# Ten instead of eight seven-product quads in each sweep of the MLPs' second weights, with one weight sum made in DRAM

## The chip, the cores and the metric

The kernel runs on one core of a Trainium2 chip. A core has engines with instruction queues of their own: TensorE (PE, matmuls; PEld in the profile are its weight loads), VectorE (DVE), ScalarE (ACT), GpSimd (POOL) and SyncE (SP), which here only issues DMAs. They wait for one another through semaphores. The metric is the device time of one launch in microseconds (us), as the median of several runs.

## The reference

A trunk of two layers on 256 positions of width 2048, in float32. Layer 0 mixes along the sequence with a convolution module, layer 1 with latent attention, and each is followed by a squared-ReLU MLP with residual add:

```python
D_MODEL, SEQ, DEPTH, D_FF = 2048, 256, 2, 8192

def sq_relu_mlp(h, w1, w2):
    return jnp.square(jax.nn.relu(h @ w1)) @ w2

# per layer: x = x + mixer(rms_norm(x)); x = x + sq_relu_mlp(rms_norm(x), w1, w2)
# at the end: rms_norm(x)
```

w1 is 2048 x 8192 and w2 8192 x 2048, so the four products of the two MLPs are most of the work, and their 256 MB of float32 weights are streamed from DRAM once.

## The kernel before

**Products of float32.** TensorE multiplies in a rounded form of float32. Each operand is therefore split: hi is its rounding, formed by ScalarE (L169 and L431), and lo what is left over, formed by VectorE as a subtraction (L173 and L432). A product is three matmuls into one PSUM bank, hi x hi, lo x hi and hi x lo (`mm3`, L202 to L204): with a stationary sh, sl of the inputs and a moving hi, lo of the weights. The third one (L204) is the first that needs the weights' lo.

**The MLP.** Its 8192 inner columns are worked off in two halves (`hf`). A half has an up stage and two sweeps. The up stage has 8 groups of 512 inner columns; for each come four loads of 1 MB of w1 (four blocks of 128 rows x 512 columns), which makes 32 loads, or steps, a half. For each block there are four pairs of matmuls (L645 with hi, L646 with lo of the weights). After each group its four PSUM banks are squared and scaled and split to hi and lo: these become the inputs of the second product. They come in one of two shapes, for plain or for mixed quads.

**The sweeps.** A sweep (`n` = 0 or 2) multiplies the half's inputs, 256 positions x 4096, with 4096 x 1024 of w2. It has 16 quads: two blocks of rows of w2 by two blocks of 512 columns, a load of 1 MB. A *plain* quad is eight products (2 rows x 2 columns x 2 position blocks), 24 matmuls. A *mixed* quad computes the same with seven products, 21 matmuls (a scheme of Strassen's kind, in Winograd's form): sums of input blocks are formed once when the group is put away (`mixed_inputs`, L453 and L459 to L462), sums of weight blocks whenever a quad is loaded (`mixed_weights`: L439 makes two 512-column sums at once, L440 and L441 one each). All seven weight blocks are split to hi and lo. The products are added up over the quads of the sweep in eight PSUM banks, four for the plain results (e) and four for mixed sums (u). `join` takes the u banks apart at the end (L522 to L525) and `close` adds the e banks to the residual xs. In the first half xs is added to by accumulating DMAs that POOL issues (L512), in the second half by VectorE (L514, L535).

**What sets the order.** In the program, groups 0, 2, 4 and 6 of each half are mixed: eight mixed and eight plain quads a sweep. `HEAD` and `TAIL` say how many plain quads come ahead of the first and after the last mixed one. Each engine runs its own queue in order; that order is fixed when the program is built, by the tile framework's scheduler, from the program's order and its buffers. The buffers are rings: three raw tiles of 1 MB for loads, which SP issues as they come free (L159), and six hi and six lo tiles of half a load each (`WB`). The inputs of the up stage lie in the tiles xt.

## Time and profile before

| | |
|---|---|
| three runs | 1942.09, 1942.22, 1942.23 us; median 1942.22 |
| span of the profiled execution | 1940.9 us |
| busy: PE, DVE, ACT, POOL | 1920.0, 1604.5, 1095.4, 241.9 us |
| mean rate of the DMA engines | 193 GB/s |
| up stage, MLP 0, first half (its end) and second half | to 478 us, 641 to 818.6 us |
| two sweeps, MLP 0, first half | 478 to 559.5 and 559.5 to 641 us |
| two sweeps, MLP 0, second half | 818.6 to 899.7 and to 980.4 us |
| two sweeps, MLP 1, first half | 1424 to 1505.5 and to 1587 us |
| two sweeps, MLP 1, second half | 1764.7 to 1846 and to 1931.5 us |

The bounds of the stages are read from the first and last matmuls of their lines and then used as windows, so they are good to some tenths of a us. In rows of the timeline the first number is the start in us from the span's start and the second the length in us; one row can stand for several instructions (x2). A length counts from an instruction's start to the end of its last write, so two that follow each other overlap a little, and what an instruction costs in a row of others is the distance of the starts. An arrow `<-` stands between the tile written and those read, and in brackets stands the idle time before an instruction with what ended it.

### The profile page before, as it was taken

To read this page: it belongs to the slowest core of one execution; us is meant where nothing else is said; L and a number is where in the kernel's file an instruction comes from. 1 tells how busy PE (TensorE), PEld (TensorE's weight loads), DVE (VectorE), ACT (ScalarE), POOL (GpSimd) and SP (SyncE) were. 2 spreads that over 40 slices of the span, in tenths; PEclk is the share of its full clock that TensorE was granted. 3 is DMA by queue.
4 is the path that set the end of the run, shared out by engine and by line. 5 is a ranking of instruction groups with operands and counts; after the bars stand their busy time and mean duration, and the time that the engine had idled before them with its cause. 6 is when DMAs were issued, how large, how long until landed. Compare 5 with 4: busy or idle time off the path is not lost. (4 is left out here: it accounts for less than half of the span.)

```text
span 1940.9 us, 28606 instructions
## 1 busy us (share of the span) xinstructions
PE 1920.0 (99%) x10799; PEld 1683.0 (87%) x10799; DVE 1604.5 (83%) x2490; ACT 1095.4 (56%) x1636; POOL 241.9 (12%) x196
## 2 busy tenths in 40 slices
PE   8999999999999999999999999999999999999997
PEld 8999888888888888888889998888888888888876
DVE  7999988877999667799976766877789986778998
ACT  5667755555565455455666565555555555555655
POOL 6999200000010000000002310000000010000000
PEclk9999999999999999999999999999999999999999
DMA  7766456555576866555665445466546786555654
GB/s 230 212 188 182 156 192 209 186 192 174 190 233 222 249 191 195 174 183 201 204 197 149 141 135 192 155 214 194 185 163 224 221 268 198 185 187 186 224 184 142
DMA packets 214571, 373.93 MB, mean 193 GB/s; under 512 B 15896, under 2 KB 90912, under 8 KB 214176
## 3 DMA queue, kind: packets, MB, share of 16 engines
q1 hardware_dynamic: 209648, 363.28, 58.1%
q0 software_dynamic: 3456, 6.29, 1.8%
q10 hardware_dynamic: 1328, 2.52, 0.4%
q8 instruction: 84, 1.38, 0.3%
q14 instruction: 55, 0.45, 0.1%
HBM read 363.68 MB, written 2.10 MB: 188 GB/s over the span
## 5 line engine op out<-in xcount | busy, mean ns | idle before, releaser
L173 DVE TENSOR_TENSOR lo<-raw,hi 128x1024 fp32r<-128x1024 f32 (+2 forms) x503 | 598.5, 1204 | 249.1 <-ACT hi L169 245.6
L169 ACT ACTIVATE hi<-raw 128x1024 fp32r<-128x1024 f32 (+1 forms) x568 | 578.8, 1038 | 357.8 <-PE acc L645 212.6
L645 PE MATMUL acc<-xt,hi 128*128 128x512 f32 x2048 | 710.5, 390 | 0.0
L646 PE MATMUL acc<-xt,lo 128*128 128x256 f32 x2048 | 577.5, 282 | 0.0
L645 PEld LDWEIGHTS acc<-xt,hi 128*128 128x128 f32 x2048 | 384.4, 188 | 80.6
L646 PEld LDWEIGHTS acc<-xt,lo 128*128 128x128 f32 x2048 | 387.1, 189 | 0.2
L431 ACT ACTIVATE hi<-raw 128x1024 fp32r<-128x1024 f32 (+1 forms) x256 | 235.6, 947 | 233.5 <-DVE raw L439 151.5
L432 DVE TENSOR_TENSOR lo<-raw,hi 128x1024 fp32r<-128x1024 f32 (+1 forms) x256 | 271.9, 1086 | 22.4 <-ACT hi L431 18.1
L204 PE MATMUL acc<-lo,sh 128*128 128x512 f32 x512 | 199.6, 390 | 1.9 <-DVE lo L432 1.9
L204 PE MATMUL acc<-lo,gh 128*128 128x512 f32 (+1 forms) x516 | 199.9, 388 | 0.8 <-DVE lo L173 0.8
L202 PE MATMUL acc<-hi,gh 128*128 128x512 f32 (+1 forms) x516 | 200.0, 388 | 0.0
L203 PE MATMUL acc<-hi,gl 128*128 128x512 f32 (+1 forms) x516 | 199.9, 387 | 0.0
L202 PE MATMUL acc<-hi,sh 128*128 128x512 f32 x512 | 199.6, 390 | 0.2 <-ACT hi L431 0.2
L788 PE MATMUL acc<-xt,hi 128*128 128x256 f32 x1024 | 180.1, 281 | 0.3 <-ACT b L1070 0.2
L203 PE MATMUL acc<-hi,sl 128*128 128x512 f32 x448 | 174.3, 389 | 0.0
L875 DVE SCALAR_TENSOR_TENSOR sum<-ub,w_dw,sum 128x256 f32<-128x256 f32 x409 | 164.2, 480 | 3.5 <-ACT sum L845 3.0
L173 POOL TENSOR_TENSOR lo<-raw,hi 128x1024 fp32r<-128x1024 f32 x65 | 155.1, 2412 | 17.3 <-ACT hi L169 17.3
L788 PEld LDWEIGHTS acc<-xt,hi 128*128 128x128 f32 x1024 | 154.6, 188 | 1.1 <-ACT xt L1054 0.6
L788 PE MATMUL acc<-xt,lo 128*128 128x256 f32 x512 | 139.2, 279 | 0.0
L512 POOL DMA_DIRECT2D xs<-v x24 | 21.1, 961 | 882.7 <-DVE lo L173 701.5
L204 PEld LDWEIGHTS acc<-lo,sh 128*128 128x128 f32 x512 | 96.1, 188 | 23.2 <-DVE lo L432 3.2
L204 PEld LDWEIGHTS acc<-lo,gh 128*128 128x128 f32 x516 | 96.8, 188 | 21.1 <-DVE lo L173 1.3
(309 smaller groups left out, 2568.2 us busy)
## 6 DMA issues: line engine op xcount, KB each, us to landing
raw<-in_mlp_w SPq DMA_DIRECT2D x256, 1024.0 KB, 5.4
raw<-in_conv_w_pw SPq DMA_DIRECT2D x62, 512.0 KB, 5.1
raw<-in_conv_w_pw SPq DMA_DIRECT2D x16, 1024.0 KB, 5.0
raw<-in_mla_w_o SPq DMA_DIRECT2D x16, 1024.0 KB, 5.4
raw<-in_mla_w_kv_up SPq DMA_DIRECT2D x8, 1024.0 KB, 5.4
xs<-v POOLq DMA_DIRECT2D x24, 256.0 KB, 7.6
raw<-in_mla_w_in SPq DMA_DIRECT2D x8, 576.0 KB, 3.8
raw<-in_mla_w_in SPq DMA_DIRECT2D x4, 1024.0 KB
```

Source lines behind the costliest of these rows:

```text
L169: nc.scalar.activation(hi, raw[:, js, :], AF.Copy)
L173: eng.tensor_tensor(lo, raw, hi.bitcast(F32), op=ALU.subtract)
L202: nc.tensor.matmul(ps, sh, mh, start=start, stop=False)
L203: nc.tensor.matmul(ps, sl, mh, start=False, stop=False)
L204: nc.tensor.matmul(ps, sh, ml, start=False, stop=stop)
L431: nc.scalar.activation(hi, src, AF.Copy)
L432: nc.vector.tensor_tensor(lo, src, hi.bitcast(F32), op=ALU.subtract)
L512: nc.gpsimd.dma_start(x, o, accum_op=ALU.add)
L645: nc.tensor.matmul(ps[b], wh[:, bs], xhl(k), start=k == 0, stop=False)
L646: nc.tensor.matmul(ps[b][:, :S], wl[:, bs], xh(k), start=False, stop=k == KC - 1)
L788: nc.tensor.matmul(pss[c][b][:, :S], w[i][:, bs], (xh, xl)[j](k), start=k == i + j == 0, stop=end and k == k0 + nk - 1 and (i, j) == terms ...
L875: nc.vector.scalar_tensor_tensor(out=out, in0=ubs[c][:, w : w + S], scalar=tap(c, w), in1=base, op0=ALU.mult, op1=ALU.add)
```

## The change

In each half groups 0, 2, 4, 6 and 7 are mixed: ten mixed and six plain quads a sweep. What goes with it:

- **Names and signs.** The four weight sums are written so that the first, q1, is the sum of the top row's two column blocks. The others follow from it: q2 = q1 + lower right, q3 = q2 - upper left, q4 = q2 + lower left (L456 to L458 in the new file, 512 columns each). The signs of the input sums and of `join` change to match.
- **q1 in DRAM.** During the first 20 of a half's 32 up steps, SP copies the right block of a quad's top row (256 KB of w2) to a DRAM tile behind the step's weight load (`issue_after`), and one step later an accumulating DMA of POOL's adds the left block. That is done for both sweeps' ten mixed quads: 80 copies and 80 accumulating DMAs in all.
- **A mixed quad's load** is three DMAs into one raw tile, 1 MB together: q1 (256 KB), the lower row (512 KB), the upper left block (256 KB). The upper right block isn't loaded.
- **Three steps.** A first half (lower right block and q1) is split as soon as its two loads are there; then upper left and lower left, and the three sums; then q2 alone, and q3 with q4. The function `run` calls the next quad's first half between the sums and the last splits of the present one. The order of the seven products changes to fit. Plain quads are cut alike, their second half being the middle step.
- **Room.** Group 7's inputs lie in the third of the xt tiles, which is now 2 MB, as the up stage needs it no more then. In each MLP's first half the tile's contents are put aside in DRAM after group 1 and brought back in the second sweep. In that sweep group 7's quads come first.
- `HEAD` is (1, 1) in place of (2, 1).

```diff
-MIXED = {(0, 0): (0, 2, 4, 6), (0, 1): (0, 2, 4, 6), (1, 0): (0, 2, 4, 6), (1, 1): (0, 2, 4, 6)}
-N_MIXED = 4
-HEAD, TAIL, LAST_TAIL = (2, 1), 2, 3
+MIXED = (0, 2, 4, 6, 7)
+IN_XT = 7
+XT_PAD = 56
+HEAD, TAIL, LAST_TAIL = (1, 1), 2, 3
...
+    dram = ctx.enter_context(tc.tile_pool(name="dram", bufs=1, space=bass.MemoryType.DRAM))
...
+    def weight_load(dst, src):
+        last_load[0] = nc.sync.dma_start(dst, src)
...
-        xt[:] = [
-            pool.tile([P, KC // NNB, 2 * S], F32R, name=nm("xt")) for _ in range(NNB)
-        ]
-    xhl = lambda k: xt[k // 4][:, k % 4, :]
+        xt[:] = [pool.tile([P, n, 2 * S], F32R, name=nm("xt")) for n in (KC // 4, KC // 4, KC // 2)]
+    def xrows(k, n):
+        i = min(k // 4, 2)
+        return xt[i][:, k - 4 * i : k - 4 * i + n, :]
...
-    def mixed_weights(raw):
-        def halves(src):
+    class MixedWeights:
+        def __init__(self, w, k, n, q1):
+            top, low = (w[(k + i) * P : (k + i + 1) * P, n * NB : (n + 2) * NB] for i in range(2))
+            raw = self.raw = wpool.tile([P, 4, NB], F32, tag="raw", name=nm("raw"), bufs=3)
+            weight_load(raw[:, 3, :], q1)
+            weight_load(raw[:, 1:3, :], low.rearrange("p (c n) -> p c n", c=2))
+            weight_load(raw[:, 0, :], top[:, :NB])
+            self.b22, self.q1 = self.halves(2, 4)
+        def halves(self, a, b):
+            src = self.raw[:, a:b, :]
             hi = wpool.tile(list(src.shape), F32R, tag="hi", name=nm("hi"), bufs=WB)
             lo = wpool.tile(list(src.shape), F32R, tag="lo", name=nm("lo"), bufs=WB)
             nc.scalar.activation(hi, src, AF.Copy)
             nc.vector.tensor_tensor(lo, src, hi.bitcast(F32), op=ALU.subtract)
-            return [(hi[:, i, :], lo[:, i, :]) for i in range(src.shape[1])]
-        b11, b21 = halves(raw[:, :, :NB])
-        (b22,) = halves(raw[:, 1:2, NB:])
-        top = raw[:, 0, :].rearrange("p (c n) -> p c n", c=2)
-        low = raw[:, 1, :].rearrange("p (c n) -> p c n", c=2)
-        nc.vector.tensor_tensor(top, raw[:, :, NB:], top, op=ALU.subtract)
-        nc.vector.tensor_tensor(low[:, 1, :], low[:, 1, :], top[:, 0, :], op=ALU.subtract)
-        nc.vector.tensor_tensor(low[:, 0, :], low[:, 0, :], low[:, 1, :], op=ALU.subtract)
-        t1, t3 = halves(top)
-        t4, t2 = halves(low)
-        return b11, b21, b22, t1, t2, t3, t4
+            return [(hi[:, i, :], lo[:, i, :]) for i in range(b - a)]
+        def sums(self):
+            raw = self.raw
+            self.b11, self.b21 = self.halves(0, 2)
+            nc.vector.tensor_tensor(raw[:, 3, :], raw[:, 3, :], raw[:, 2, :], op=ALU.add)
+            nc.vector.tensor_tensor(raw[:, 0, :], raw[:, 3, :], raw[:, 0, :], op=ALU.subtract)
+            nc.vector.tensor_tensor(raw[:, 1, :], raw[:, 3, :], raw[:, 1, :], op=ALU.add)
+        def rest(self):
+            (self.q2,) = self.halves(3, 4)
+            self.q3, self.q4 = self.halves(0, 2)
+    class PlainWeights:
+        def __init__(self, w, k, n):
+            self.raw = load([rows(w, k, 2, n * NB, 2 * NB)], 2)
+            self.parts = [split_half(self.raw, 0, nc.vector)]
+        def sums(self):
+            self.parts.append(split_half(self.raw, 1, nc.vector))
+        def rest(self):
+            pass
+        def at(self, j):
+            return [a[:, 0, :] for a in self.parts[j]]
...
-        def mixed(self, w, k, fh, fl, end):
-            b11, b21, b22, t1, t2, t3, t4 = mixed_weights(load([rows(w, k, 2, self.n * NB, 2 * NB)], 2))
+        def mixed(self, b, fh, fl, end):
             u1, u6, u7, u5 = self.u
             work = [
-                (u1, 0, b11), (u5, 6, t1), (u7, 4, t3), (u6, 3, t2),
-                (self.e[0][0], 1, b21), (self.e[0][1], 5, b22), (self.e[1][0], 2, t4),
+                (self.e[0][1], 5, b.b22), (u5, 6, b.q1), (u1, 0, b.b11), (self.e[0][0], 1, b.b21),
+                (u6, 3, b.q2), (u7, 4, b.q3), (self.e[1][0], 2, b.q4),
             ]
-            if self.begun:
-                work = [work[i] for i in (0, 4, 5, 1, 2, 6, 3)]
             for ps, i, (wh, wl) in work:
                 mm3(ps, fh[:, i, :], fl[:, i, :], wh, wl, self.first(ps), end and any(ps is u for u in self.u))
...
+                ms = [(g, b) for g in mixed for b in range(2)]
+                sums_due = [(n, i) for n in range(0, NNB, 2) for i in range(len(ms))]
+                first_sums, half_done = {}, []
...
+                        while half_done:
+                            q1, src = half_done.pop(0)
+                            nc.gpsimd.dma_start(q1, src, accum_op=ALU.add)
+                        if sums_due:
+                            n, i = key = sums_due.pop(0)
+                            k = k_lo + 4 * ms[i][0] + 2 * ms[i][1]
+                            q1 = first_sums[key] = dram.tile([P, NB], F32, name=nm("q1"))
+                            row = w[k * P : (k + 1) * P, n * NB : (n + 2) * NB]
+                            with tc.issue_after(last_load[0].ins):
+                                nc.sync.dma_start(q1, row[:, NB:])
+                            half_done.append((q1, row[:, :NB]))
...
+                    if not last and g == 1:
+                        spare = dram.tile([P, KC // 2, 2 * S], F32, name=nm("spare"))
+                        nc.sync.dma_start(spare, xt[2].bitcast(F32))
...
+                    if g == IN_XT:
+                        room_x = xt[2].rearrange("p k n -> p (k n)")[:, XT_PAD : XT_PAD + 4 * 7 * P]
+                        gs[g] = [a.rearrange("p (b i n) -> p b i n", b=2, i=7) for a in (room_x[:, : 14 * P], room_x[:, 14 * P :])]
...
-                    g, b = ms[i]
-                    sums.mixed(w, k_lo + 4 * g + 2 * b, gs[g][0][:, b], gs[g][1][:, b], i == len(ms) - 1)
+                    n = sums.n
+                    at = i if n == 0 else (i - 2) % len(ms)
+                    g, b = ms[at]
+                    return (
+                        lambda: MixedWeights(w, k_lo + 4 * g + 2 * b, n, first_sums[n, at]),
+                        lambda q: sums.mixed(q, gs[g][0][:, b], gs[g][1][:, b], i == len(ms) - 1),
+                    )
+                def plain_quad(sums, k, at_end):
+                    def middle():
+                        while due:
+                            prepare(due.pop(0))
+                    return (
+                        lambda: PlainWeights(w, k_lo + k, sums.n),
+                        lambda q: sums.plain(q, hi, lo, k, at_end, middle if at_end else None),
+                    )
+                def run(units):
+                    quads = [u for u in units if isinstance(u, tuple)]
+                    begun = [quads[0][0]()]
+                    for u in units:
+                        if not isinstance(u, tuple):
+                            u()
+                            continue
+                        q = begun.pop()
+                        q.sums()
+                        quads.pop(0)
+                        if quads:
+                            begun.append(quads[0][0]())
+                        q.rest()
+                        u[1](q)
...
+                        if not last and n == NNB - 2 and i == len(ks) // 2:
+                            units.append(lambda: nc.sync.dma_start(xt[2].bitcast(F32), spare))
                         if i == len(ks) - tail + 1:
-                            sums.join(room)
-                        at_end = i == len(ks) - 1
-                        sums.plain(
-                            w, k_lo + k, hi, lo, k, at_end,
-                            (lambda: [prepare(due.pop(0)) for _ in range(len(due))]) if at_end else None,
-                        )
+                            units.append(lambda: sums.join(room))
+                        units.append(plain_quad(sums, k, i == len(ks) - 1))
                     if ends:
-                        while at < len(ms):
-                            mixed_quad(sums, at)
-                            at += 1
+                        units += [mixed_quad(sums, i) for i in range(at, len(ms))]
+                    run(units)
...
```

VectorE's order shows the weights of one mixed quad. Before, in the first half's first sweep of MLP 0 (raw_5649 is the quad's load; hi and lo are its split blocks):

```order
L432 TENSOR_TENSOR lo_5652<-raw_5649,hi_5651 128x1024
L432 TENSOR_TENSOR lo_5656<-raw_5649,hi_5655 128x512
L439 TENSOR_TENSOR raw_5649<-raw_5649 128x1024
L440 TENSOR_TENSOR raw_5649<-raw_5649 128x512
L441 TENSOR_TENSOR raw_5649<-raw_5649 128x512
L432 TENSOR_TENSOR lo_5663<-raw_5649,hi_5662 128x1024
L432 TENSOR_TENSOR lo_5667<-raw_5649,hi_5666 128x1024
```

Now, in the same sweep (raw_5716 is the quad, raw_5755 the next one, raw_5799 a plain one behind it):

```order
L450 TENSOR_TENSOR lo_5721<-raw_5716,hi_5720 128x1024
L450 TENSOR_TENSOR lo_5749<-raw_5716,hi_5748 128x1024
L456 TENSOR_TENSOR raw_5716<-raw_5716 128x512
L457 TENSOR_TENSOR raw_5716<-raw_5716 128x512
L458 TENSOR_TENSOR raw_5716<-raw_5716 128x512
L450 TENSOR_TENSOR lo_5760<-raw_5755,hi_5759 128x1024
L450 TENSOR_TENSOR lo_5764<-raw_5716,hi_5763 128x512
L450 TENSOR_TENSOR lo_5768<-raw_5716,hi_5767 128x1024
L450 TENSOR_TENSOR lo_5793<-raw_5755,hi_5792 128x1024
L456 TENSOR_TENSOR raw_5755<-raw_5755 128x512
L180 TENSOR_TENSOR lo_5802<-raw_5799,hi_5801 128x1024
```

Before, the quad's rows stand together. Now lo_5760, the next quad's first half, stands between its sums and its last two splits; three steps of 1024 columns are left (with L439 there were four) and four of 512 (there were three).

Behind the other kind of neighbour, a few quads on, the quad's own rows close up (raw_5755 of above, raw_5838 the next mixed one):

```order
L457 TENSOR_TENSOR raw_5755<-raw_5755 128x512
L458 TENSOR_TENSOR raw_5755<-raw_5755 128x512
L450 TENSOR_TENSOR lo_5806<-raw_5755,hi_5805 128x512
L450 TENSOR_TENSOR lo_5810<-raw_5755,hi_5809 128x1024
L180 TENSOR_TENSOR lo_5835<-raw_5799,hi_5834 128x1024
L450 TENSOR_TENSOR lo_5843<-raw_5838,hi_5842 128x1024
```

Here the 1024-column split, which reads what L457 and L458 write, follows L458 with only one 512-column row between.

SP's queue in the up stage of MLP 0's first half, before only the loads of L159, now (q_ are the DRAM sums, spare the tile put aside):

```order
L157 DMA raw_4047<-in_mlp_w 128x4x512
L691 DMA q_510_4090<-in_mlp_w 128x512
L157 DMA raw_4092<-in_mlp_w 128x4x512
L691 DMA q_516_4135<-in_mlp_w 128x512
L697 DMA spare_4227<-xt_100 128x4096
L157 DMA raw_4137<-in_mlp_w 128x4x512
L691 DMA q_522_4180<-in_mlp_w 128x512
```

A copy now stands behind each load, and once the 2 MB going out.

43 lines of the change are left out of this document (23 added, 20 removed).

## The prediction

> **What bounds the kernel now.** The kernel's profiled execution has a span of 1940.9 us, and the runs have a median of 1942.22 us, so 1.3 us lie around the span. I make the sum as a difference and add it to the median. The first view read is the page's table of busy times, and after it a table of stretches: the two sweeps of MLP 0's first half, the up stage and the two sweeps of its second half, and the kernel's last two sweeps. The columns are the length, then busy time of PE, PEld, DVE, ACT and POOL (with instructions), the granted clock, the DMA share and GB/s.
>
> ```profile
> PE 1920.0 (99%) x10799; PEld 1683.0 (87%) x10799; DVE 1604.5 (83%) x2490; ACT 1095.4 (56%) x1636; POOL 241.9 (12%) x196
> 478.00:559.50 81.50, 81.50 (x362) 67.52 (x361) 76.84 (x85) 45.93 (x53) 3.64 (x4) 1.00 0.60 194
> 559.50:641.00 81.50, 81.50 (x362) 67.49 (x361) 76.44 (x80) 46.97 (x52) 5.22 (x6) 1.00 0.74 236
> 641.00:818.60 177.60, 177.60 (x1026) 157.40 (x1025) 124.97 (x185) 90.02 (x127) 1.77 (x2) 1.00 0.64 200
> 818.60:899.70 81.10, 81.10 (x360) 67.17 (x359) 78.44 (x89) 45.71 (x53) 0.10 (x1) 1.00 0.56 189
> 899.70:980.40 80.70, 79.94 (x352) 65.53 (x351) 78.32 (x92) 46.08 (x57) 0.15 (x1) 1.00 0.60 198
> 1764.70:1846.00 81.30, 81.30 (x361) 67.35 (x360) 78.46 (x89) 45.18 (x52) 0.00 (x0) 1.00 0.60 201
> 1846.00:1931.50 85.50, 83.26 (x375) 68.09 (x373) 82.41 (x103) 47.50 (x62) 0.00 (x0) 1.00 0.47 159
> ```
>
> TensorE is the bound, at full clock. But the average of 83% for VectorE hides that in a sweep it works 76.4 to 78.5 us of 81.5: only 3 to 5 us are free. In the up stage it is free for 50 us of 177.6. So a cut of TensorE's sweeps is worth its full size only while VectorE keeps up. The timeline of TensorE shows where it already doesn't: single matmuls around the gaps in the second halves' second sweeps (start, length, and in brackets the idle time with its releaser).
>
> ```profile
> 912.09 0.39 PE L203 MATMUL acc<-hi,sl 128*128 128x512 f32 x1
> 912.32 0.39 PE L204 MATMUL acc<-lo,sh 128*128 128x512 f32 x1
> ...
> 914.20 0.50 PE L204 MATMUL acc<-lo,sh 128*128 128x512 f32 x1 [0.70 <-DVE lo L432]
> 914.54 0.40 PE L202 MATMUL acc<-hi,sh 128*128 128x512 f32 x1
> ...
> 1858.37 0.39 PE L204 MATMUL acc<-lo,sh 128*128 128x512 f32 x1
> ...
> 1860.69 0.40 PE L202 MATMUL acc<-hi,sh 128*128 128x512 f32 x1
> 1875.22 0.39 PE L203 MATMUL acc<-hi,sl 128*128 128x512 f32 x1
> 1876.14 0.50 PE L204 MATMUL acc<-lo,sh 128*128 128x512 f32 x1 [0.54 <-DVE lo L432]
> 1876.48 0.40 PE L202 MATMUL acc<-hi,sh 128*128 128x512 f32 x1
> 1922.11 0.39 PE L204 MATMUL acc<-lo,gh 128*128 128x512 f32 x1
> 1923.32 0.73 PE L204 MATMUL acc<-lo,gh 128*128 128x512 f32 x2 [0.83 <-DVE lo L173]
> 1923.89 0.40 PE L202 MATMUL acc<-hi,gh 128*128 128x512 f32 x1
> ```
>
> Matmuls of 512 columns start 0.226 us apart where nothing waits (81.5 us over 360 of them; 912.09 to 912.32). From 912.32 to 914.54 four steps took 2.22 us instead of 0.91: 1.3 lost. In the last sweep 1858.37 to 1860.69 lost 1.4, 1875.22 to 1876.48 lost 0.8, and 1922.11 to 1923.89 1.1. In all 4.6 us, each after a late lo of VectorE.
>
> **Term 1: matmuls.** Ten quads of 21 matmuls and six of 24 make 354 where eight and eight made 360: 6 fewer, 6 x 0.2264 = 1.36 us per sweep, and 8 sweeps give **-10.9 us**. A sweep falls to 80.1 us.
>
> **Term 2: VectorE's weights.** The timeline of VectorE over one mixed and one plain quad, in a sweep in which it hardly waits:
>
> ```profile
> 847.38 1.22 DVE L439 TENSOR_TENSOR raw<-raw 128x1024 f32<-128x1024 f32 x1
> 848.63 0.69 DVE L440 TENSOR_TENSOR raw<-raw 128x512 f32<-128x512 f32 x1
> 849.35 0.69 DVE L441 TENSOR_TENSOR raw<-raw 128x512 f32<-128x512 f32 x1
> 849.96 2.52 DVE L432 TENSOR_TENSOR lo<-raw,hi 128x1024 fp32r<-128x1024 f32 x2
> 852.40 2.35 DVE L173 TENSOR_TENSOR lo<-raw,hi 128x1024 fp32r<-128x1024 f32 x2
> 854.67 1.82 DVE L432 TENSOR_TENSOR lo<-raw,hi 128x1024 fp32r<-128x1024 f32 x2
> 856.40 1.22 DVE L439 TENSOR_TENSOR raw<-raw 128x1024 f32<-128x1024 f32 x1
> L431 ACT ACTIVATE hi<-raw 128x1024 fp32r<-128x1024 f32 x192 | 200.9, 1057 | 230.6 <-DVE raw L439 151.5 <-DVE raw L441 33.7 <-PE acc L203 24.2
> ```
>
> A plain quad takes 2.27 us (852.40 to 854.67, so 1.14 a subtraction of 1024), a mixed and a plain one 9.02 (847.38 to 856.40), so the mixed one 6.75; a 512-wide step takes 0.6 (1.73 - 1.14). A mixed quad of the change has three of 1024 and four of 512: 3 x 1.14 + 4 x 0.60 = 5.82. The wait inside it is added: the last pair's hi (1.06 on ScalarE, last row above) starts only after the third addition, and where just the 512-wide subtraction stands between, VectorE idles about 0.7. In the order of the change that holds for about three quads of ten, and two or three more have an addition right behind the one whose result it reads (0.72 instead of 0.60, as 848.63 to 849.35). With smaller gaps elsewhere I take 0.29 a quad as the mean: 6.1. (The old quad, counted so, is 3 x 1.14 + 0.6 + 1.14 + 2 x 0.6 = 6.36 against 6.75 measured, a wait of 0.39.) A sweep then costs 10 x 6.1 + 6 x 2.27 = 74.6 us against 8 x 9.02 = 72.2: **+2.4 us of VectorE**, between -0.4 (no waits) and +4.6 (0.5 a quad).
>
> So a sweep in which VectorE was busy 78.4 of 81.1 now has 80.8 of 79.7; in the first halves, whose results POOL's DMAs add, it is 79.2 of 80.1. VectorE's lead over TensorE shrinks by 1.36 + 2.4 = 3.8 us a sweep. It is made good in the up stage (over 50 us free there), so each pair of sweeps starts with a full lead and the question is where it is used up. VectorE also has group 7's inputs to form at the start of each first sweep, from this row and its three neighbours (L460 to L462, alike):
>
> ```profile
> L453 DVE TENSOR_TENSOR sl<-v,sh 128x128 fp32r<-128x128 f32 (+1 forms) x96 | 44.2, 463 | 0.5
> L459 DVE TENSOR_TENSOR v<-v 128x128 f32<-128x128 f32 x32 | 9.1, 284 | 0.1
> L673 DVE TENSOR_TENSOR gl<-v,gh 128x512 fp32r<-128x512 f32 x32 | 21.8, 684 | 0.0
> ```
>
> Each of the group's two pairs of blocks costs 3 x 0.46 + 4 x 0.28 instead of 0.68, 1.8 more: +3.6 us, just when the lead is being spent. Here is how little of it was left in the first half, 32 us into its first sweep:
>
> ```profile
> 509.23 2.52 DVE L432 TENSOR_TENSOR lo<-raw,hi 128x1024 fp32r<-128x1024 f32 x2
> 511.07 0.39 PE L204 MATMUL acc<-lo,sh 128*128 128x512 f32 x1
> ```
>
> The first of that pair was done at about 510.45 (half-way), its reader started at 511.07: 0.6 us of room. I took both engines' orders of the change and added row upon row, with these steps: the nearest point moves to 15 us into the sweep (the third mixed quad, behind one plain one where there were two), where the row sum is 0.8 short and about 1.9 with the waits. So **1.9 us** of stall in each first half. In the second halves the loss up to 912 is 3.8 x 94/81 = 4.4 on top of 1.3: 5.7 at most; row by row I get **4.3**. In the last pair 3.3 are lost before, and up to 3.8 x 158/81 = 7.4 come on top; row by row **7.2**. Together 2 x 1.9 + 4.3 + 7.2 = 15.3 us against 4.6: **+10.7**. Without the waits the same addition gives 3.7 (0.8 + 0.8 + 0 + 2.1), with 0.5 a quad and a later load for the next quad's first half some 22.
>
> **Term 3: sums in DRAM.** In 20 of each half's 32 up steps, behind the 1 MB load, SP issues a 256 KB copy and, one step later, POOL an adding DMA of 256 KB. POOL is idle there (1.8 us of 177.6) and nothing but these DMAs is queued behind its wait. SP waits nowhere new. What they cost is time of the DMA engines, which no row shows for DRAM to DRAM. The nearest are the DMA view for 641 to 660 us, where the old kernel's adding DMAs (q0) run beside loads (q1), then that for 700 to 800 us without them:
>
> ```profile
> q1 hardware_dynamic: 2206, 4.36, 64.5%
> q0 software_dynamic: 573, 1.04, 30.6%
> raw<-in_mlp_w SPq DMA_DIRECT2D x3, 1024.0 KB, 7.0
> ...
> q1 hardware_dynamic: 9249, 18.88, 60.8%
> raw<-in_mlp_w SPq DMA_DIRECT2D x18, 1024.0 KB, 5.3
> ```
>
> A packet of the loads took 0.645 x 16 x 19 / 2206 = 0.089 us, of the additions 0.306 x 16 x 19 / 573 = 0.162. A step lasts 177.6 / 32 = 5.55 us, of which loads take 0.608 x 5.55 = 3.4. A 256 KB DMA is 128 rows of 2 KB, 8 packets per engine: 0.71 us at the one price, 1.30 at the other, 2.6 at twice the latter. Low: 3.4 + 0.7 + 1.3 = 5.4, hidden. Middle, taken: 3.4 + 1.3 + 1.3 = 6.0, so 20 x 0.4 = 8 us late, which three loads waiting in the raw ring and a VectorE ahead by two to three loads (about 17 us) hide, and 12 steps without sums win back. High: 3.4 + 1.3 + 2.6 = 7.3, 35 us late, of which some 17 would show, per half. I take **0**.
>
> By the Trainium skill ("Collectives: The Full Stack", the section on the bandwidth ceiling and the fold count), an adding transfer reads two sources and so moves at half a copy's rate. The two packet times, 0.162 against 0.089, agree: 1.8. By that rule a sum costs 0.7 + 1.4 us of a step, 5.5 in all, and the low end would hold.
>
> **Term 4: xt's third tile.** 2 MB go out near the end of group 1 and come back in the first half's second sweep, ahead of weight loads on SP's queue. At the loads' 3.4 us per MB that is 6.7 us each way. The way out delays loads by that once, inside the 17 us above. On the way back the next load comes 5 to 7 us later, and the room there is VectorE's lead (over 5 us by the row sums in that sweep) and the filled raw ring: between 0 and 3 us, twice, 0 taken.
>
> **Sum:** -10.9 + 10.7 + 0 + 0 = -0.2, so **1942 us**: TensorE's matmuls give, VectorE's lateness takes.
>
> **The rivals.**
> *A: VectorE keeps up.* If the waits don't arise (the next quad's first half fills them) stalls are 3.7 us, and the time is 1942.2 - 10.9 - 0.9 = 1930.4; with half the waits 1936. For it: in the first halves 2 us stay free even by my count. Against it: the gaps at 912 and 1858, with no room left.
> *B: DMA becomes the bound of the up stage.* From 6.4 us per step (20 x 0.85 = 17) TensorE waits for weights; at 6.7 each half loses 6, and 24 us make 1966; at the high end 17 x 4 = 68 make 2010. For it: loads took 7.0 instead of 5.3 us where additions ran beside. Against it: the DMA share in the up stage is 0.64. The Trainium skill ("DMA: Bandwidth & Descriptors", the section on issuing engines not being separate queues) says that DMAs share the 16 engines whichever engine starts them; the 7.0 us agree, so POOL's queue is no way round SP's loads.
> *C: late weights in the sweeps.* A mixed quad's first half needs two of three loads; where a plain quad gives the raw ring only 2.27 us of VectorE, they can come 0.5 us late (5.3 us of landing against some 5 to 6.5 of work). Ten quads' waits of 0.5 and the reload's 3 us give 22.4 + 6 us of stalls in place of 15.3: 1955.
> *D: the order undoes it.* If reordered rows put a late mixed quad before ready plain work, stalls move and don't shrink; within C's price.
>
> **How the numbers follow.** What a measurement tells from no change is about 0.2%, 3.9 us. The forecast's case (1937 to 1948) gets 0.40: 0.28 inside 0.2%, 0.05 faster, 0.07 slower. A gets 0.32, faster. C and D get 0.18 and B 0.10, slower. So faster 0.37, same 0.28, slower 0.35. The range leaves out the last of A below 1930 (0.06) and of B and C above 1960 (0.13); the forecast's own is 1937 to 1948.
>
> **What would show it.** Right: TensorE busy in a sweep falls to about 80.1 us; VectorE's busy time in a second half's sweep rises to 80 or more; L204 waits for lo of L450 add up to about 15 us, most in the last two sweeps; a mixed quad takes 6.1 us of VectorE. Wrong for A: waits under 5 us. For B: in an up stage TensorE waits on hi or lo behind DMA raw, and the up stages last over 178 us. For C: ACT hi waits for DMA raw inside the sweeps, above all behind the reload.

## The result, and the profile after

The changed kernel took **2001.51 us** (median of five runs, 1998.33 to 2006.61), the one before 1942.22: a ratio of 1.0306, 95% interval 1.0293 to 1.0318. Slower, by 59 us, where 1942 had been forecast and 1930 to 1960 given as the range.

The length of each stage of the two MLPs, from its first matmul to the next stage's first (the second halves' sweeps of MLP 0 have the attention layer behind them, as far as MLP 1):

| us | MLP 0, first half: up | sweeps | second half: up | sweeps and attention | MLP 1, first half: up | sweeps | second half: up | sweeps |
|---|---|---|---|---|---|---|---|---|
| before | 177.7 | 163.2 | 177.5 | 427.6 | 177.7 | 163.2 | 177.5 | 167.0 |
| after | 185.9 | 173.8 | 179.6 | 433.7 | 189.2 | 175.8 | 180.0 | 172.0 |

The up stages lost 24.3 us, 19.7 of them in the first halves, and the sweeps 34.3, although they have 10.9 us of matmuls less. The page's table of busy times of the changed kernel, two of its DMA queues, and the table of stretches (length, busy time of PE, PEld, DVE, ACT and POOL, granted clock, DMA share, GB/s) for the stages that answer to those shown of before:

```profile
PE 1942.9 (97%) x10751; PEld 1666.2 (83%) x10751; DVE 1625.4 (81%) x2618; ACT 1117.5 (56%) x1684; POOL 308.1 (15%) x276
...
q1 hardware_dynamic: 234544, 392.66, 60.1%
q0 software_dynamic: 14976, 27.27, 8.0%
...
300.60:486.50 185.90, 180.22 (x1027) 159.35 (x1026) 140.94 (x245) 95.20 (x140) 13.95 (x17) 0.98 0.81 244
486.50:573.40 86.90, 85.28 (x365) 66.59 (x364) 76.94 (x102) 50.20 (x61) 3.54 (x4) 1.00 0.58 182
573.40:660.40 87.00, 83.34 (x348) 63.32 (x347) 76.77 (x88) 47.17 (x53) 5.26 (x6) 1.00 0.72 229
660.40:840.00 179.60, 177.86 (x1026) 157.36 (x1025) 128.96 (x192) 90.31 (x130) 18.31 (x22) 1.00 0.88 264
840.00:923.60 83.60, 81.91 (x352) 64.14 (x351) 78.60 (x106) 48.32 (x59) 0.10 (x1) 1.00 0.55 180
923.60:1007.00 83.40, 81.91 (x350) 63.72 (x349) 79.53 (x99) 50.04 (x63) 0.15 (x1) 1.00 0.59 193
1902.00:1990.00 88.00, 85.05 (x368) 65.76 (x367) 84.84 (x109) 49.78 (x65) 0.00 (x0) 1.00 0.50 162
```

Two things are to be seen. VectorE is busy 78.6 and 79.5 us of 83.5 in the sweeps of MLP 0's second half, where it was 78.4 and 78.3 of some 81; what grew most is the time that it idles in a sweep that is now longer. And the granted clock fell to 0.98 over a whole up stage.

**In the sweeps**, the view of waits over the whole run (engine and line, what it waited for: us in total, times, the longest), first of before and then of after:

```profile
ACT hi L169 <- DMA raw<-in_mlp_w: 20.9, 9, 3.2
ACT hi L431 <- DMA raw<-in_mlp_w: 6.7, 4, 3.0
```

```profile
ACT hi L176 <- DMA raw<-in_mlp_w: 133.9, 49, 11.8
...
ACT hi L449 <- DMA raw<-in_mlp_w: 82.0, 27, 5.8
...
DVE lo L450 <- ACT hi L449: 46.7, 56, 4.7
```

The mixed quads' splits wait for their loads 27 times, where they did 4 times, for 82 us in place of 7. (L176 is the line of the plain quads and of the up stages; 88 of its 134 us lie in the second halves' up stages, where TensorE hardly waited.) VectorE waits in turn for the hi. The timeline of VectorE in the first sweep, with the two kinds of wait side by side:

```profile
504.81 0.68 DVE L458 TENSOR_TENSOR raw<-raw 128x512 f32<-128x512 f32 x1
505.41 0.68 DVE L450 TENSOR_TENSOR lo<-raw,hi 128x512 fp32r<-128x512 f32 x1
506.70 1.23 DVE L450 TENSOR_TENSOR lo<-raw,hi 128x1024 fp32r<-128x1024 f32 x1 [0.61 <-ACT hi L449]
...
528.25 0.69 DVE L458 TENSOR_TENSOR raw<-raw 128x512 f32<-128x512 f32 x1
530.46 4.10 DVE L450 TENSOR_TENSOR lo<-raw,hi 128x1024 fp32r<-128x1024 f32 x4 [1.53 <-ACT hi L449]
```

The 0.61 us at 506.7 are those that the forecast had counted (about 0.7): q3 and q4's hi can start only after L458. The 1.53 us before 530.46 are another kind. The next quad's first half was due, and ScalarE's timeline shows that it waited 4.19 us for that quad's load.

**In the first halves' up stages** one stall does it, 29 us into the stage. Timelines of ScalarE, VectorE and TensorE there:

```profile
327.19 1.06 ACT L176 ACTIVATE hi<-raw 128x1024 fp32r<-128x1024 f32 x1 [8.82 <-DMA raw<-in_mlp_w]
328.16 0.92 ACT L715 ACTIVATE v<-acc 128x256 f32<-128x256 f32 x3
```

```profile
317.38 2.36 DVE L180 TENSOR_TENSOR lo<-raw,hi 128x1024 fp32r<-128x1024 f32 x2
328.28 1.23 DVE L180 TENSOR_TENSOR lo<-raw,hi 128x1024 fp32r<-128x1024 f32 x1 [8.54 <-ACT hi L176]
329.43 1.08 DVE L716 TENSOR_TENSOR v<-acc,v 128x256 f32<-128x256 f32 x3
```

```profile
329.90 0.79 PE L679 MATMUL acc<-xt,hi 128*128 128x512 f32 x1 [5.68 <-DVE v L716]
330.49 0.41 PE L680 MATMUL acc<-xt,lo 128*128 128x256 f32 x1
330.70 0.63 PE L679 MATMUL acc<-xt,hi 128*128 128x512 f32 x1
```

It reads from top to bottom: ScalarE waits 8.8 us for a load, and VectorE 8.5 us for its hi. The emptying of group 0's PSUM banks needs neither, but it stands behind them in both queues: ScalarE's copy of one part (L715) behind the late hi, VectorE's addition of the other (L716), which reads that copy, behind the late lo. TensorE needs these banks and waits 5.7 us. In MLP 1 the same wait was 8.8 us. The DMA view for 312 to 334 us shows how late the loads were, 13.3 us to landing instead of 5.3, beside sums and the 2 MB going out:

```profile
raw<-in_mlp_w SPq DMA_DIRECT2D x4, 1024.0 KB, 13.3
spare<-xt SPq DMA_DIRECT2D x1, 2048.0 KB
q<-in_mlp_w SPq DMA_DIRECT2D x3, 256.0 KB, 13.4
q<-in_mlp_w POOLq DMA_DIRECT2D x3, 256.0 KB, 6.6
```

### The profile page after: what moved, and what is told of

Its sections match the earlier page's. It is cut to its first block, busy times and chain, and to the rows that moved or that the text cites. A ratio compares the mean times of both kernels' runs of the same rounds, so it can differ in the third digit from the quotient of the medians.

```text
span 2000.6 us, 29263 instructions
## 1 busy us (share of the span) xinstructions
PE 1942.9 (97%) x10751; PEld 1666.2 (83%) x10751; DVE 1625.4 (81%) x2618; ACT 1117.5 (56%) x1684; POOL 308.1 (15%) x276
## 3 DMA queue, kind: packets, MB, share of 16 engines
q0 software_dynamic: 14976, 27.27, 8.0%
## 5 line engine op out<-in xcount | busy, mean ns | idle before, releaser
L180 DVE TENSOR_TENSOR lo<-raw,hi 128x1024 fp32r<-128x1024 f32 (+2 forms) x471 | 560.6, 1203 | 246.4 <-ACT hi L176 241.0
L176 ACT ACTIVATE hi<-raw 128x1024 fp32r<-128x1024 f32 (+2 forms) x536 | 545.7, 1037 | 377.9 <-PE acc L679 135.8
L449 ACT ACTIVATE hi<-raw 128x1024 fp32r<-128x1024 f32 (+1 forms) x320 | 290.3, 945 | 256.1 <-DVE raw L458 89.9
L450 DVE TENSOR_TENSOR lo<-raw,hi 128x1024 fp32r<-128x1024 f32 (+1 forms) x320 | 336.8, 1087 | 48.2 <-ACT hi L449 46.7
L211 PE MATMUL acc<-lo,sh 128*128 128x512 f32 x512 | 189.8, 399 | 5.5 <-DVE lo L450 5.4
L209 PE MATMUL acc<-hi,gh 128*128 128x512 f32 (+1 forms) x388 | 150.7, 388 | 0.0
L210 PE MATMUL acc<-hi,gl 128*128 128x512 f32 (+1 forms) x388 | 150.2, 388 | 0.0
L684 POOL DMA_DIRECT2D q<-in_mlp_w x80 | 66.7, 834 | 538.4 <-DMA q<-in_mlp_w 509.9
L211 PE MATMUL acc<-lo,gh 128*128 128x512 f32 (+1 forms) x388 | 147.2, 388 | 2.5 <-DVE lo L180 2.5
L209 PEld LDWEIGHTS acc<-hi,sh 128*128 128x128 f32 x512 | 96.1, 188 | 43.7 <-ACT hi L449 25.5
```

The source lines that it names most:

```text
L176: nc.scalar.activation(hi, raw[:, js, :], AF.Copy)
L180: eng.tensor_tensor(lo, raw, hi.bitcast(F32), op=ALU.subtract)
L209: nc.tensor.matmul(ps, sh, mh, start=start, stop=False)
L210: nc.tensor.matmul(ps, sl, mh, start=False, stop=False)
L211: nc.tensor.matmul(ps, sh, ml, start=False, stop=stop)
L449: nc.scalar.activation(hi, src, AF.Copy)
```

## The experiments

### What of the loss belongs to which part

Three kernels take parts of the change away. The tile put aside (e1):

```diff
-                    if not last and g == 1:
-                        spare = dram.tile([P, KC // 2, 2 * S], F32, name=nm("spare"))
-                        nc.sync.dma_start(spare, xt[2].bitcast(F32))
...
-                            units.append(lambda: nc.sync.dma_start(xt[2].bitcast(F32), spare))
```

> Edit: the third xt tile is neither put aside in DRAM nor brought back (the second half's up stage then reads group 7's inputs in its place, so its numbers are not the reference's). The changed kernel is 58.2 us longer than the one before in the profiled spans: up stages of the first halves +8.2 and +11.4, of the second halves +2.1 and +2.4, sweeps of the first halves +10.5 and +12.7, of the second halves about +5.5 and +5.0. Theory 1 (the 2 MB transfer out holds the DMA engines when they are already full, and one stall of TensorE of 5.7 and 8.9 us comes of it): the first halves' up stages fall to the second halves' 180 us, about -16 in all, and the way back costs at most 4 more: 1981 to 1986 us. Rival (the 20 sums alone fill the engines and the transfer out only shows where the backlog breaks): at most half of the stall goes, 1990 to 1996.

Measured: 1987.08 us, 14.4 less than the changed kernel. First halves' up stages 178.2 and 179.8 (from 185.9 and 189.2), their sweeps 173.8 and 176.4 (from 173.8 and 175.8). So the transfer out is most of those stages' loss, as theory 1 has it, though the time lies 1 us above its range; the transfer back costs nothing that shows.

The sums in DRAM (e2, which loads the upper right block into q1's place):

```diff
-            weight_load(raw[:, 3, :], q1)
+            weight_load(raw[:, 3, :], top[:, NB:])
...
-                            nc.gpsimd.dma_start(q1, src, accum_op=ALU.add)
...
-                                nc.sync.dma_start(q1, row[:, NB:])
```

> Edit: no copy and no adding DMA; a mixed quad's q1 place is loaded with the upper right block straight from w2, 256 KB as before (its sums are then not the reference's). Theory 1: the second halves' up stages are back at 177.6 us (-4.5 in all), and in the first halves the 2 MB transfer out is hidden with the sums gone (-15 or more), sweeps as they are: about 1980. Rival (the transfer out stalls by itself): the first halves' up stages keep 5 us or more each, 1987 to 1992. If the sweeps too get faster by over 5 us, the sums' DRAM tiles or late adding DMAs cost something there, which neither theory has.

Measured: 1997.51. First halves' up stages 180.0 and 184.8: the transfer out alone costs 2.3 and 7.1, sums alone (e1) 0.5 and 2.1, both together 8.2 and 11.5. The time lies outside both ranges. By the up stages the rival was nearer: 2 MB at once do stall by themselves, and with the sums it is worse than the two added. The sweeps got 8.6 us longer, which hides most of the gain in the total.

Both (e3), which leaves the sweeps as the only difference to the kernel before:

> Both edits at once. All up stages should be as in the kernel before (177.6 us each), and what is left is the sweeps alone: if nothing of the up stages reaches into them, +34 us against the kernel before, about 1976. If the sweeps' late weights come from DMA traffic left over from the up stages or from the transfer back, they shrink too: 1955 to 1965.

Measured: 1987.15. All up stages are back at 177.7 and 177.5, but the sweeps are not shorter: 964.5 us in all (attention included), against 955.3 in the changed kernel and 921.0 before. That they are 9 us longer than with the sums in DRAM was not expected and stays open. One candidate is q1's source: the load of q1 from its DRAM tile landed in 2.7 us in the changed kernel, the 256 KB loads from w2 in 4.9 here. The loss of the sweeps, in any case, is made in the sweeps.

The new quads, but eight of them, with HEAD (2, 1) and no tile put aside (e4):

```diff
-MIXED = (0, 2, 4, 6, 7)
+MIXED = (0, 2, 4, 6)
```

> Edit: the new quads (three steps, sums in DRAM) with eight mixed ones as before (groups 0, 2, 4, 6), two plain quads ahead, no tile put aside; the result is the reference's. VectorE's work per sweep falls by 8 x 0.65 = 5 us against the kernel before, TensorE's is the same 81.5. If the sweeps of the change are slow for VectorE's own steps and waits, these are gone: sweeps at 81.5, the 4.6 us of stalls of the kernel before gone too, up stages of +2 each: 1941 to 1946. If they are slow for weights that land too late in a ring of three loads, two mixed quads in a row still wait: stalls of 3 us or more a sweep, 1955 to 1970.

Measured: 1949.08, between the two expectations: sweeps of 164.7, 431.1, 164.4 and 167.3. VectorE was busy 73.2 to 73.3 us in a first sweep of MLP 0, where it was 76.8 and 78.4 before, and yet the sweeps got no shorter: VectorE idled 7 to 16 us in each, and the splits waited for loads much longer than before (in the whole run the mixed quads' by L449 48 us, where it was 7, and those by L176, of plain quads and up stages, 205, where it was 21).

### The ring of three

A raw tile is taken when a quad's load is issued and given back when its last split is done. With the change a quad's first half is split before the quad ahead has had its last splits, so two quads hold tiles while the third is being loaded. The DMA engines could have carried more: in e3's sweeps of MLP 0's second half their share was 0.54 and 0.59. Three experiments on the base of e3. The next quad's first half later (e5):

```diff
                         q.sums()
+                        q.rest()
                         quads.pop(0)
                         if quads:
                             begun.append(quads[0][0]())
-                        q.rest()
```

> Base: the run without sums in DRAM and without the tile put aside (1987.15 us), so only sweeps differ. Edit: the next quad's first half is called after the present quad's last splits, not before them. Theory R (a ring of three loads is too short: a quad's slot is held from the next quad's early first half until its own last splits, so the load that follows starts late): slots come free one first half (1.14 us) and more earlier, waits of ScalarE for DMA raw in the sweeps fall by over half; the waits for L458 rise to about 0.6 us at each of ten quads, so the gain is partly spent: 1970 to 1987. Rival V (VectorE's own steps and its waits on its own sums set the pace): seven more waits of 0.6 us a sweep, 4 us x 8, 2010 to 2020.

Measured: 1984.73, 2.4 less. Within R's bounds, at their upper end. The view of waits over the whole run (in e3 the two rows were 80.6 us, 27 times, and 50.3 us, 58 times):

```profile
ACT hi L449 <- DMA raw<-in_mlp_w: 2.2, 2, 1.4
...
DVE lo L450 <- ACT hi L449: 45.3, 71, 0.9
```

So the loads of the mixed quads are in time even with three tiles when tiles are given back sooner, and the gain is spent at once: VectorE's few long waits have become many short ones behind its own sums. A fourth raw tile, with the early first half kept and the final gain loaded later (e6):

```diff
+    def quad_raw(shape):
+        quads_no[0] += 1
+        if quads_no[0] % 4 == 0:
+            return extra[0].tile(shape, F32, tag="raw4", name=nm("raw"), bufs=1)
+        return wpool.tile(shape, F32, tag="raw", name=nm("raw"), bufs=3)
...
+            raw = self.raw = quad_raw([P, 4, NB])
...
-            gfs.append(mp.tile([P, D], F32, name="gf"))
+            gfs.append(wpool.tile([P, D], F32, tag="raw", name="gf", bufs=3))
```

> Same base (1987.15). Edit: the quads of the sweeps use four raw tiles in turn, the fourth in room that the final gain had; the gain is loaded later, into the ring, behind the last weight load. Theory R: waits for DMA raw in the sweeps go, 2 to 5 us of VectorE's idle time a sweep with them, and what they push back: 1950 to 1965. Rival V: VectorE has as much to do, at most 1 us a sweep: 1979 to 1987.

Measured: 1951.59, **35.6 us less**, as R had it. The view of waits in the sweeps of MLP 0's second half, of e3 and then of e6 (where L449 has become L458):

```profile
ACT hi L449 <- DMA raw<-in_mlp_w: 26.6, 8, 4.3
ACT hi L449 <- DVE raw L458: 22.2, 12, 2.7
DVE lo L450 <- ACT hi L449: 10.6, 12, 1.6
```

```profile
ACT hi L458 <- DVE raw L467: 26.4, 14, 2.7
ACT hi L458 <- PE acc L210: 12.6, 8, 2.4
...
DVE lo L459 <- ACT hi L458: 2.9, 6, 0.6
```

One wait of a mixed quad for a load is left, of 2.0 us, and some splits now wait for TensorE to free a hi tile, the sign of an engine that is ahead. VectorE's waits for hi fall from 10.6 to 2.9 us, 7.7; the stage got 9.4 us shorter. In the first of the two sweeps VectorE was busy 77.67 us of 83.5 in e3 and is busy 80.67 of 82.5 in e6: it has hardly any idle time left.

The additions left out (e7):

```diff
-            nc.vector.tensor_tensor(raw[:, 3, :], raw[:, 3, :], raw[:, 2, :], op=ALU.add)
-            nc.vector.tensor_tensor(raw[:, 0, :], raw[:, 3, :], raw[:, 0, :], op=ALU.subtract)
-            nc.vector.tensor_tensor(raw[:, 1, :], raw[:, 3, :], raw[:, 1, :], op=ALU.add)
```

> Same base. Edit: the three 512-column additions of a mixed quad's weights (L456 to L458) are left out, so q2 to q4 are not the reference's; everything else stays. VectorE's work falls by 10 x 1.8 = 18 us a sweep and the waits for L458 go. Theory V: sweeps are bound by TensorE alone, 80.1 us each: 1927 to 1933. Theory R (late loads hold the pace, and the slots' time is mostly the load's own 5.3 us and the wait for the next quad): at least a third of the 43 us stays, 1945 to 1965.

Measured: **1924.90**, 17.8 under the kernel before and a little under V's bounds, although the ring has three tiles. The table of stretches for two of its sweeps:

```profile
478.70:559.00 80.30, 80.30 (x355) 66.47 (x355) 65.23 (x78) 51.59 (x61) 3.62 (x4) 1.00 0.67 205
816.70:896.00 79.30, 79.30 (x352) 65.64 (x351) 66.43 (x82) 51.61 (x62) 0.10 (x1) 1.00 0.64 202
```

TensorE is busy from end to end, with VectorE at 65 and 66 us. The splits still waited 82 us for loads in that run, but VectorE had room to make it good. So R and V are not rivals: the late loads cost time because VectorE is full, and VectorE being full costs less when loads are in time. Against e7's sweeps (904.4 us in all) e6's 929.1 are still 24.7 longer: this is the additions with the waits behind them, and e3's further 35.4 is what the fourth tile takes away. The two shares depend on the order in which they are taken: on the ring of three, leaving out the additions alone took off all 60.

The early first half, with loads in time (e11; the edit of e5 on the base of e6):

> Base: the four-tile run without sums and tile put aside (1951.59). Edit: the next quad's first half after the present quad's last splits. With a ring of three this edit gained 2.4 us. Theory: it gained there only because slots came free earlier; with loads in time what is left is the added wait for L458, 0.6 us at seven more quads a sweep of a VectorE that is nearly full: 1957 to 1975. Rival (the early first half is of no use with any ring): 1945 to 1952.

Measured: 1984.11, 32.5 *more* than e6, beyond the theory's range. The early first half is worth 32 us with four tiles and less than nothing with three. With the last splits first the fourth tile itself is worth 0.6 us (e5 took 1984.73), and VectorE's waits for hi are e5's over again, 71 times and 45.1 us, where e6 has 36 and 22.6. So the two go together: the early first half saves the waits behind the sums, and only the fourth tile keeps it from being paid for in late loads. In MLP 0's second half VectorE's idle time grew by 6.2 us (two thirds of it waits for sums of its own) and the stage by 9.4; the rest is not accounted for.

### The transfer out and the sums

The line that puts the tile aside was moved behind group 5 (e9):

```diff
-                    if not last and g == 1:
+                    if not last and g == 5:
```

> Base: the changed kernel (2001.51). Edit: the third xt tile is put aside after group 5, when the 20 sums are done, and not after group 1 among them; the result is the reference's. Theory (the transfer out and the sums together are too much, each nearly fits): the first halves' up stages fall from +8.2 and +11.4 us to what they were without the tile put aside, +0.4 and +2.0: 1982 to 1987. Rival (2 MB at once behind the loads stall by themselves, as the run without sums had with +2.2 and +7.0): 1990 to 1994.

Measured: 2000.10, no change, and outside both ranges. This told nothing of the theory, since the transfer hadn't moved. SP's timeline of the changed kernel and of e9:

```profile
312.83 0.36 SPq L697 DMA_DIRECT2D spare<-xt  x1
```

```profile
312.60 0.35 SPq L697 DMA_DIRECT2D spare<-xt  x1
```

The scheduler issued it at the same place wherever it was written; it needs only xt. With four tiles as well, and so the whole change with one tile more (e10):

> The run before this one with four raw tiles in turn for the quads, everything else of the change kept (ten mixed quads, sums in DRAM, the tile out and back); the result is the reference's. If the two causes found (a short ring, the transfer out among the sums) are all that there is, its time is that of the four-tile run without sums (1951.59) plus the 7 us that the up stages keep: 1953 to 1961. If the sums' tiles or the transfer back cost something in the sweeps once loads are in time, more: 1962 to 1970.

Measured: 1968.08. That lies in the second range, but not for its reason. The sweeps took 930.6 us in all, as in e6 (929.1), so the sums' tiles and the transfer back cost next to nothing there; the transfer out had stayed where it was, and the up stages kept more than the 7 us. Against the changed kernel (955.3) the fourth tile takes 24.7 us off the sweeps. The second halves' up stages took 177.5, with all sums beside them: **hidden entirely**. The first halves' took 187.6 and 186.3, 18.5 us more than before.

Then the transfer was tied behind group 5's last load, as the copies are tied to theirs (e13):

```diff
-                        nc.sync.dma_start(spare, xt[2].bitcast(F32))
+                        with tc.issue_after(last_load[0].ins):
+                            nc.sync.dma_start(spare, xt[2].bitcast(F32))
```

> Base: four raw tiles with everything of the change kept (1968.08). In that run and the one before it, moving the line that puts the tile aside to group 5 moved nothing: the scheduler issued the transfer at the same place of SP's queue, among the sums, 313 us into the span. Edit: it is tied behind the last weight load of group 5 (as the sums' copies are tied to theirs), so it stands behind the 20 sums. Theory (the transfer out and the sums together are too much): the first halves' up stages fall from 187.7 and 186.4 to about 178, 1968 - 17 = 1949 to 1953. Rival (2 MB at once stall by themselves, as without the sums, +2.2 and +7.0): 1957 to 1962.

Measured: 1961.47, up stages of 182.8 and 179.8. The time lies in the rival's range, but the rival's reason does not hold: the transfer now left at 409 us, in a stretch without a stall. What is left in the first of these stages is a stall of 3.3 us at 328 us, where sums alone ran beside the loads, so the theory failed too: the sums stall there without the transfer. On top of it, the e banks added by DMA (e14):

```diff
-                    if c == 0 or not self.by_dma:
+                    if not self.by_dma:
```

> The run before this one, and in the first halves the e banks of a sweep's first column block too are added to xs by accumulating DMAs (ScalarE copies them, POOL issues), where VectorE added them and waited 3 to 5 us a time for the mixed sums' DMAs into the same places. If that wait is what keeps the first halves' second sweeps long: 4 to 8 us less than the run before, 1942 to 1948. If not (the banks then come free no sooner, as the same DMAs stand ahead on POOL's queue): within 2 us of it.

Measured: 1960.39, within the runs' scatter of e13. The first halves' sweeps got 2.2 us shorter in all, the up stages behind them 3.1 longer: VectorE's wait for those DMAs isn't what keeps the first halves' sweeps long. Last, the sums from group 2 on and the transfer behind group 6 (e15):

```diff
-                        if sums_due:
+                        if sums_due and g >= 2:
...
-                    if not last and g == 5:
+                    if not last and g == 6:
```

> Base: four raw tiles with the transfer out tied behind group 5 (1961.47). There the first halves' up stages still took 183 and 180 us, with a stall of TensorE 28 us into the stage, where only sums ran beside the loads. Edit: the 20 sums begin with group 2, 44 us later, and the 2 MB go out behind group 6. Theory (the cushion of loads and split weights isn't there yet at a stage's start; later on the sums are hidden): up stages of all halves at 177.7, and the whole 7 us less: 1952 to 1956. Rival (the sums stall wherever they begin): 1959 to 1964.

Measured: **1952.87**. The table of stretches over the first up stage:

```profile
300.30:478.00 177.70, 177.70 (x1026) 157.56 (x1025) 140.89 (x244) 94.66 (x138) 16.55 (x20) 1.00 0.86 265
```

TensorE has no gap, with a DMA share of 0.86 where 0.81 went with the stall. So it is not how much the DMA engines carry over the stage, but what they carry in its first 30 us. With that, 10 us of loss remain against the kernel before. All of it lies in the first halves' sweeps (167.7 and 169.6, where they were 163.2); those of the second halves are 0.5 us shorter than before each.

### A version that is a little faster than both

The first experiments pointed to eight mixed quads in the new form with the last splits first (e8; the edit of e5 on the base of e4):

> Base: the run with eight mixed quads (1949.08), the result the reference's. Edit: the next quad's first half after the present quad's last splits. VectorE there idled 8 to 15 us a sweep for late loads, with 5 us less work than in the kernel before. Theory R: the late loads shrink, VectorE keeps its lead, stalls fall under 2 us in all: 1941 to 1945. Rival V: eight waits of 0.6 us on L458 a sweep are added and nothing is won: 1949 to 1955.

Measured: **1939.66**, a ratio of 0.9984 to the kernel before (1942.67 in these runs), interval 0.9975 to 0.9993. That is 1.3 us better than R's range and clear of the runs' scatter, but it is less than the 0.2% that the prediction set as the least that tells anything. The table of stretches over the sweeps of MLP 0's second half:

```profile
819.00:900.00 81.00, 81.00 (x359) 67.07 (x358) 73.95 (x89) 46.50 (x53) 0.10 (x1) 1.00 0.56 189
900.00:981.00 81.00, 81.00 (x368) 67.31 (x367) 74.18 (x93) 46.82 (x59) 0.15 (x1) 1.00 0.59 196
```

The stall at 912 us is gone: VectorE is at 74 us, where it was at 78.4. A ninth mixed quad in the second halves on top (e12):

```diff
-                ms = [(g, b) for g in mixed for b in range(2)]
+                ms = [(g, b) for g in mixed for b in range(2)] + [(IN_XT, 0)] * last
```

> Base: the run with eight mixed quads and the last splits first (1939.66). Edit: nine mixed quads in each sweep of the second halves, the ninth's inputs in the third xt tile, which no later stage needs there (nothing is put aside), the final gain loaded late into the ring; the result is the reference's. TensorE: 3 matmuls fewer in four sweeps, 4 x 0.68 = 2.7 us. If VectorE's room there (2 to 3 us a sweep of waits for TensorE to free hi and lo, and the lead out of the up stage) holds 3.8 us more work a sweep: 1936 to 1938. If not, TensorE waits 1 to 3 us a sweep: 1940 to 1947.

Measured: 1949.94, worse than both ranges. Sweeps and attention took 430.0 in place of 424.9, the last sweeps 169.2 in place of 167.9; some 3 us more lie ahead of the first MLP and behind the last matmul. In the first of these sweeps VectorE was busy 77.05 us of 82.6 and waited 4.9 more for ScalarE's hi, so hardly any room was left. One quad was too much.

## Why the prediction was wrong

**Term 1 (matmuls, -10.9) was right.** In e7, where VectorE has room, the sweeps with attention are 904.4 us against 921.0: 10.9 of matmuls, the 4.6 of old stalls, and 1 more.

**Term 2 (VectorE) had the steps right, and failed in "With smaller gaps elsewhere I take 0.29 a quad as the mean" and in the 15.3 us that the row sums made of it.** By the starts of L456 in the first sweep (511.25, 518.13, 526.92 and 534.48 us) a mixed quad costs VectorE 5.9 to 6.0 us without its waits, where 5.82 had been taken. The counted wait was 0.61 us, mostly three times a sweep, as forecast. What was missing is the loads. VectorE's waits for the mixed quads' hi came to 46.7 us, 0.58 a quad, in the changed kernel, and to 22.7, 0.28 a quad, in e10, where loads are in time: the mean was that of a kernel without late loads. VectorE's idle time behind late loads was 1.3 to 4.8 us in each of the eight sweeps; it belonged to rival C, which I had priced at 22.4 us of stalls and kept apart from the forecast's case. They are not apart: a sweep whose VectorE has 80.8 us of work and waits in 79.7 (the forecast's own figures, and 3.6 of group 7's inputs on top in each first sweep, which that line left out) has no room for an idle microsecond.

The sweeps took 34.3 + 10.9 = 45 us more than their matmuls account for, where 10.7 had been set. Of these the fourth tile takes 24.7 off (e10), and 20.5 stay with loads in time, so the row sums were too low by some 10 us as well. They failed in the first halves: -10.9/4 + 1.9 = -0.8 us had been forecast for each, and in e10 they are 4.6 and 5.9 longer than before, while the second halves came out 0.8 and 1.6 us better than forecast. What makes the first halves' sweeps long stays open; by e14 it is not VectorE's wait for POOL's DMAs.

The step behind the late loads was the diff read without the ring. I priced a load at 0.5 us late, and only outside the forecast's case, in rival C. What the change does to the ring is that a quad's tile is taken up by its early first half while the quad ahead still holds its own until its last splits, so of three tiles one is left for loading. Both ways out of it bring the loads in time, tiles given back sooner (e5) and a fourth tile (e6, e10), and only the second also saves the waits behind the sums.

**Term 3 (sums in DRAM at 0) was right of the second halves once the loads of the sweeps are in time:** their up stages took 177.5 us in e10. In the changed kernel they took 2.1 and 2.5 us more, with one stall of 1.7 and one of 1.9 us, each 5 us into the stage. In the first halves the sums alone cost 0.5 and 2.1 us (e1) and 5.1 and 2.1 (e13), at the stage's start. The prices can now be read. An adding packet took 0.080 x 16 x 2000.6 / 14976 = 0.171 us (0.162 before), as taken. A copy is no dearer than a load: in the DMA view for 700 to 720 us, where loads and copies share the queue, a packet took 0.759 x 16 x 20 / 2641 = 0.092 us.

```profile
q1 hardware_dynamic: 2641, 5.15, 75.9%
q0 software_dynamic: 495, 0.91, 27.3%
...
raw<-in_mlp_w SPq DMA_DIRECT2D x4, 1024.0 KB, 12.8
```

So a step is 3.4 + 0.7 + 1.4 = 5.5 us, near the low end, and not the middle of 6.0 that I reckoned with. That is also what the Trainium skill's rule gave ("Collectives: The Full Stack", the section on the bandwidth ceiling and the fold count). Full engines still showed in the landing, 12.8 us instead of 5.3, and in the second halves it was hidden.

**Term 4 (the tile put aside at 0) failed in "near the end of group 1" and in "inside the 17 us above".** The transfer left 12 us into the stage, in group 0, and the 17 us of cushion were worked out for a stage under way. There was none yet: the load that came late was issued at 313.97 us, and ScalarE was free for it at 318.4, 4.4 us later, where a load alone takes 5.3. And the place where the lateness hurts was not the matmul that needs the load but the emptying of group 0's banks, which stands behind that load's hi on ScalarE and its lo on VectorE. I had named what waits behind SP and POOL, not behind these two. The first halves' up stages lost 19.7 us; without the transfer (e1) they lose 2.6 and without the sums (e2) 9.4, so most of it took both. e15, in which sums and transfer both start later, gives all of it back.

**The rivals.** B named the right stage, but not what happened in it: by the prices above a step's DMA work stayed at 5.5 us, under B's 6.4, and the loss was one stall at the start of each first half, not a little at every step. C's mechanism was right and its price far too low. Both came, and I had given them 0.18 and 0.10 as if only one could. A was wrong of the changed kernel; where VectorE does keep up, as in e7 without the additions, the time was 1924.9, beside A's 1930.4.

**What would show it:** I had expected VectorE's busy time in a second half's sweep to rise to 80 or more; it was 78.6 and 79.5. My 80.8 had counted 2.9 us of waits as busy, and what came on top was idle time. ScalarE's waits for raw inside sweeps, named as C's sign, were there.

## What to carry to other kernels

When a change splits a unit of work into early and late parts, count for each buffer from when it is taken to when it is given back: a ring can get shorter without its number changing, and an engine that is nearly full has no way to make late loads good. A cushion has to be read at the place where it is used: the first 30 us of a stage are not its middle, and what comes too late may be an instruction that merely stands behind the late one in a queue. And a line's place in the program is no promise of its place in a queue where a scheduler decides; the order has to be looked at again after the edit.

## What the runs showed of the hardware that was not expected

A gap of TensorE costs more than its length. After the 5.7 us stall the first matmuls of 512 columns took 0.63 us and the 256-wide ones 0.41, where 0.39 and 0.28 are usual. The table of stretches around it:

```profile
318.00:324.00 6.00, 6.00 (x37) 5.25 (x36) 1.74 (x2) 0.38 (x1) 0.00 (x0) 1.00 0.99 320
324.00:330.00 6.00, 0.32 (x3) 0.10 (x1) 1.72 (x3) 2.81 (x6) 0.81 (x1) 0.83 1.04 352
330.00:336.00 6.00, 6.00 (x22) 5.15 (x23) 5.14 (x11) 2.13 (x6) 0.83 (x1) 0.60 1.05 257
336.00:342.00 6.00, 6.00 (x37) 5.33 (x36) 5.29 (x12) 3.15 (x5) 1.21 (x2) 1.00 0.93 257
```

The granted clock was 0.60 for the next 6 us, and 22 matmuls ran where 37 do: some 2.4 us lost again, and the stage took 8.2 us longer for a stall of 5.7. The stalls in the changed kernel's sweeps were at most 1.6 us each and left the clock at 1.00, as did the one of 1.9 us in its last up stage. One of 2.06 us in e3, in a sweep of MLP 1's first half, did not; the row of the timeline, and the table of stretches right behind it:

```profile
1536.73 0.50 PE L211 MATMUL acc<-lo,gh 128*128 128x512 f32 x1 [2.06 <-DVE lo L180]
```

```profile
1537.70:1541.10 3.40, 3.40 (x9) 2.63 (x9) 3.40 (x5) 1.69 (x2) 1.10 (x2) 0.50 0.93 285
```

e15 shows the same, 3.4 us at 0.50 behind a stall of 2.27. The Trainium skill ("TensorE: Matmul & The Clock Gate", the section on the clock gate) says that the clock is halved after an idle window of about 3.4 us and full again after about 3.4 us of sustained work. The halving and the 3.4 us at half speed agree with these traces; the idle time does not, as 2.06 and 2.27 us were enough.
